# Moving the high parts of the weight ring, and the latents, by fractions of 256 bytes

## The chip, the cores and the metric

The kernel runs on one core of one Trainium2 chip. The metric is device time in microseconds (us) of one execution; lower is better. The time of a kernel is the median of its runs. The engines are named as in the profile: PE does the matmuls (PEld is its weight load), DVE, ACT and POOL are the vector, scalar and GpSimd engines, SP issues DMAs.

## The reference, cut to what matters

Two layers over 256 positions of width 1024. Layer 0 has latent attention, layer 1 has sparse attention over keys and values computed once between the layers. After each attention comes a PEER block: every position picks experts out of 16384 by product keys, and sums their outputs.

```python
def mla_mixer(x, ...):
    c_q  = rms_norm(proj[..., :512], q_norm)        # the latents
    c_kv = rms_norm(proj[..., 512:768], kv_norm)
    q, kv = c_q @ w_q_up, c_kv @ w_kv_up            # heads from the latents
    ...
def peer_ffn(x, w_q, subkeys, u, v):                # once in each layer
    q = x @ w_q                                     # 1024 -> 2048
    experts, g = top16(q, subkeys)                  # of 16384, 8 heads
    a = gelu(u[experts] . x)
    return sum(g * a * v[experts])
```

## The kernel before

**Arithmetic.** A float32 weight is used as the sum of a high part `hi` (float32 rounded to the format that PE multiplies in one pass, `F32R`) and a low part `lo = raw - hi`; so is the activation. A product is three matmuls: high by high, high by low, low by high.

**The stream.** All weights that pass through PE stand in one list, `plan()` (L50), in the order of use, as pieces of 128 rows by 1024 columns (the first eight by 800): projections of layer 0, then for each layer the queries of the PEER block (`p_wq`, 16 pieces), `p_u` (128 pieces) and `p_v` (128 pieces), and between the layers the weights of layer 1's attention. SP loads a piece into one of four places `raw` (in the v stage of both layers also into four places `spare`, which lie where the activations `hT` were). `_shi` (L111) lets ACT copy it into the next of four places of the ring `hi`, and `_slo` (L122) lets DVE subtract, into the next of four places of the ring `lo`. `nxt` hands the two to the matmuls; ACT and DVE work two pieces ahead of PE. Some pieces don't use the ring, but tiles of their own called `keep`.

**The stages of PE.** In the projections and in the *u stage* the weights are the stationary operand: `proj_T` (L198) runs, for each piece, 8 + 8 matmuls with blocks of 128 columns of `hi` and 8 with blocks of `lo`, against 256 columns of the activations `hT` as the moving operand. A u step (`u_step`, L708) does that for one piece. Once the expert choice is done (`if not side and len(A) == 1:`, L790), its buffers are freed, and the rest of the u steps are *wide*: 8 matmuls with `hi` against 512 columns (high and low half of `hT` in one), and 8 with `lo` against 256. There are 41 narrow and 87 wide steps in each layer. In the *v stage* the weights move (512 columns of `hi` or `lo`), and the gated activations `W` are stationary. Weights move also in the first projection, in the output projections (against `oT`), and in the first query pieces of each PEER block (against `hT`, `early_mm`). In `mla`, `proj_T` runs 192 matmuls of 256 columns with the latents `cT` as the moving operand.

**Where the tiles lie.** Tiles are laid one behind another in each partition's memory, each rounded up to 32 bytes, pool after pool. A place of the `hi` ring is 4096 bytes, and the four of them lie directly ahead of the four of `lo`. So modulo 256 bytes the starts are these: `hT` and `spare` 96; `raw`, all places of `hi`, all of `lo`, `W`, and the `keep` tiles of the v stage 160; the latents `cT`, and `qT`, `kT`, `vN`, `oT` of layer 0's attention 160; `oT` of layer 1's attention 224. All blocks that a matmul reads begin a multiple of 256 bytes behind these starts. Below, the *distance* of a matmul is the start of its moving operand less that of its weights, modulo 256: -64 for `hT` against `hi` or `lo`, 0 for `cT` against `hi`, 0 for `hi` against `W`, +64 where `hi` or `lo` moves against `hT`.

**The gather.** For 64 of the 256 positions, the last step of PEER is not done by PE: POOL gathers rows of `p_v` and DVE sums them in `g_mac` (L479), with the products of gate and activation in `gw`, made from `ggate`.

Of the kernel before, what the change touches and what calls it, by code (L numbers as in the profile page):

```python
# [12 lines left out]
F32 = mybir.dt.float32  # L13
F32R = mybir.dt.float32r
# [10 lines left out]
P = 128  # L25
# [18 lines left out]
class Kern:  # L44
# [5 lines left out]
    def plan(self):  # L50
        I, L = self.I, []
        self.v0s, self.spare, self.pairs = [], None, {}
        if "mla" in self.parts:
            L += [I["a_w_in"][k] for k in range(KC)]
            L += [I["a_wk"][i] for i in range(2)]
            L += [I["a_wq"][i] for i in range(3)]
            L += [I["a_wv"][i] for i in range(2)]
            L += [I["a_wq"][i] for i in range(3, 6)]
            L += [I["a_wo"][i] for i in range(KC)]
        for l in (0, 1):  # L60
            if l == 1 and "nsa" in self.parts:
                L += [I["s_wv"][i] for i in range(4)]
                L += [I["s_wT"][i] for i in range(4)]
                L += [I["b_wg"]]
                L += [I["s_wT"][i] for i in range(4, 8)]
                L += [I["b_wq"][i] for i in range(4)]
                L += [I["b_wq"][i] for i in range(4, 8)]
                L += [I["b_wo"][i] for i in range(KC)] + [I["b_wo"][i] for i in range(KC // 2)]
            if f"peer{l}" in self.parts:
                L += [I["p_wq"][l, i] for i in range(16)]  # L70
                L += [I["p_u"][l, (P - FIRST + j) % P] for j in range(P)]
                self.v0s.append(len(L))
                o = (len(L) - self.v0s[0]) % 4
                self.pairs.update((len(L) + j, I["p_v"][l, j:j + 2].rearrange("j i d -> i j d")) for j in range(o % 2, P - 1, 2))
                L += [I["p_v"][l, j] for j in range(P)]
        self.stream = L
        self.v0 = self.vb = self.v0s[0]
        self.si = 0
        self.sd = 0
        self.sh = 0  # L80
        self.sl = 0
        self.raws, self.his, self.los = {}, {}, {}
        self.share = False
        self.alt = {}
        self.later, self.now = [], 0
# [25 lines left out]
    def _shi(self, upto):  # L111
        while self.sh <= min(upto, len(self.stream) - 1):
            i = self.sh
            self._sdma(i, True)
            if i in self.alt:
                self.his[i], self.los[i] = self.alt.pop(i)()
            else:
                self.his[i] = self.shl.tile([P, self.raws[i].shape[-1]], F32R, tag="hi", name="hi")
            self.nc.scalar.copy(self.his[i], self.raws[i])  # L119
            self.sh += 1  # L120

# [320 lines left out]
    def peer(self, l):  # L442
        tc, nc, I = self.tc, self.nc, self.I
        self.v0 = self.v0s.pop(0)
        with ExitStack() as es:
# [14 lines left out]
            gat = pool(es, "gather")  # L460
            gidx = gat.tile([P, 2, P // 2], U32, name="gidx")
            ggate = gat.tile([P, P // 2], F32, name="ggate")
            gw = gat.tile([P, P // 2], F32, name="gw")
            gel = [gat.tile([P, 4], F32, name=f"gel{m}") for m in range(16)]
            gacc = gat.tile([P, D], F32, name="gacc")
            grow, gtable = {}, I["p_v"].rearrange("l j i d -> (l j i) d")
# [164 lines left out]
            def g_flush(n=1):  # L631
                if len(gq) < n:
                    return
                while gq:
                    t0, oi, gs = gq.popleft()
                    ps = self.acc(t0 // 4 % 2)
                    for q in range(4):
                        for w in range(2):
                            self.mm(ps[:, q * P:(q + 1) * P], oi[:, q // 2, :, q % 2], gs[w][:, q // 2, :, q % 2],
                                    w == 0, w == 1)  # L640
                    pv = ps.rearrange("p (t j) -> p j t", t=4)
                    k = done["a"]
                    for x, j0, n in A:
                        m = min(max(k, 0), n)
                        if m > 0:
                            y = x[:, 0:m, t0:t0 + 4]
                            nc.vector.scalar_tensor_tensor(y, pv[:, j0:j0 + m], 1.0 / GS, y, op0=OP.mult, op1=OP.mult)  # L647
                        if m < n:
                            nc.scalar.activation(x[:, m:n, t0:t0 + 4], pv[:, j0 + m:j0 + n], AF.Copy, scale=1.0 / GS)
                        k -= n  # L650
                    done["g"] = t0 + 4
# [41 lines left out]
            for n in range(4, 17):  # L693
                cur = []
                if n < 16:
                    hi, lo = self.nxt()
# [18 lines left out]
            def u_step(j):  # L715
                hi, lo = self.nxt()
                ps = self.ps()
                wide = len(A) > 1
                if wide:

                    def high(k):
                        self.mm(ps, hi[:, k * P:(k + 1) * P], self.hTT[:, k].rearrange("p a t -> p (a t)"), k == 0, k == KC - 1)

                    for k in range(KC - 1):
                        high(k)
                    for k in range(KC):
                        self.mm(ps[:, 0:S], lo[:, k * P:(k + 1) * P], xhi[:, k, :], False, False)
                    high(KC - 1)
                else:
                    self.proj_T(ps[:, 0:S], hi, lo, xhi, xlo, KC)  # L730
                return j, ps, wide
# [4 lines left out]
            def u_fin(x):  # L736
                while due:
                    y, ps = due.popleft()
                    nc.vector.tensor_tensor(y, y, ps, op=OP.mult)
                if x is None:  # L740
                    return
                j, ps, wide = x
                jj = (P - FIRST + j) % P
                y, n = slot(jj), done["g"]
                if wide:
                    t = gat.tile([P, S], F32, tag="half", name="half", bufs=2)
                    nc.scalar.copy(t, ps[:, S:2 * S])  # L747
                    nc.vector.tensor_tensor(ps[:, 0:S], ps[:, 0:S], t, op=OP.add)  # L748
                if n:
                    nc.scalar.activation(ps[:, 0:n], ps[:, 0:n], AF.Gelu)  # L750
                    due.append((y[:, 0:n], ps[:, 0:n]))
                if n < ND:
                    nc.scalar.activation(y[:, n:ND], ps[:, n:ND], AF.Gelu)  # L753
                if j % 4 == 0:
                    gst.append(gat.tile([P, 4, GT], F32, tag="gst", name="gst", bufs=2))
                nc.scalar.activation(gst[-1][:, j % 4, :], ps[:, ND:S], AF.Gelu)  # L756
                if j % 4 == 3:
                    nc.gpsimd.dma_start(self.actD[:, jj - 3:jj + 1, :], gst.pop())  # L758
                done["a"] = j + 1
# [24 lines left out]
            for j in range(P):  # L784
                x = u_step(j)
                u_fin(pu)
                pu = x
                g_flush(2)
                run_side(1.6 if len(A) == 1 else GB)
                if not side and len(A) == 1:  # L790
                    es_r.close()
                    hot = self.pr8.tile([P, 2, 3, 2, P, 2], F16, tag="r8", name="hot")
                    A.append((self.pr8.tile([P, NEXT, ND], F32, tag="r8", name="A2"), 0, NEXT))
                    n = P - FIRST - NEXT
                    A.append((pool(es_1, "slots1").tile([P, n, ND], F32, name="A1"), NEXT, n))
                    side.append(g_gen(hot))
                if done["g"] == ND and j >= P - 3 and not W:
                    w_start()
# [44 lines left out]
            for j in range(P):  # L843
# [9 lines left out]
                hi, lo = self.nxt(j < P - 2)  # L853
# [54 lines left out]
    def mla(self, hN, gb):  # L908
# [3 lines left out]
        with es:  # L912
            pool = lambda *a, **k: es.enter_context(tc.tile_pool(*a, reuse_waits="tile", **k))
            mp = pool(name="mla", bufs=1)
# [2 lines left out]
            keep = pool(name="mkeep", bufs=4)  # L917
            cN = mp.tile([P, 2, 768], F32, name="cN")
            kpN = mp.tile([P, 2, 32], F32, name="kpN")
            cT = [mp.tile([P, 6, S], F32R, tag=f"cT{i}", name=f"cT{i}") for i in range(2)]  # L920
            qT = mp.tile([96, NH, S], F32, name="qT")
            kT = mp.tile([96, NH, S], F32, name="kT")
            vN = mp.tile([P, 2, D], F32, name="vN")
            oT = [mp.tile([P, KC, S], F32R, tag=f"oT{i}", name=f"oT{i}") for i in range(2)]
            gq = mp.tile([P, 6], F32, name="gq")
            rN = mp.tile([P, 2, 64], F32, name="rN")
# [9 lines left out]
            for k in range(KC):  # L936
                hi, lo = self.nxt(k <= KC - 3)
# [66 lines left out]
            for b in range(2):  # L1004
                hi, lo = self.nxt(False)
# [14 lines left out]
            for b in range(2):  # L1020
                hi, lo = self.nxt()
# [21 lines left out]
            for k in range(2):  # L1043
                hi, lo = self.nxt()
# [14 lines left out]
            for st in range(NH + 3):  # L1059
# [20 lines left out]
                if 0 <= h < NH and h % 2 == 1:  # L1080
                    pvp = self.ps()
                    pp = [pts.pop(h - 1), pts.pop(h)]
                    for w in range(2):
                        for e in range(2):
                            o = pvp[64 * e:64 * e + 64, 0:S]
# [578 lines left out]
```

## Time and profile before

| what | us |
|---|---|
| median of 3 runs | 1758.89 (1757.74 to 1759.99) |
| the profiled execution | 1749.82 |
| its span, first to last instruction | 1748.0 |
| PE busy in it | 1703.1 (97%) |
| DVE busy | 1553.4 (89%) |
| ACT busy | 1042.9 (60%) |
| POOL busy | 481.4 (28%) |

The profiled execution is 9.1 us shorter than the median, and 1.8 us of it lie outside its span. A duration of a matmul in the profile is from its start to its end, and matmuls overlap: what one of them costs is the time from its start to the start of the next, its *pitch*. It is read from the timeline or the chain as the difference of two starts, divided by the number of matmuls between them.

### The profile page before, as it was taken

The numbers are of one execution on the slowest core, as the hardware profiler recorded it, in microseconds if no ns is written. First come the engines' busy times: TensorE is split into PE (matmuls) and PEld (weight loads), VectorE is DVE, ScalarE is ACT, GpSimd is POOL, SyncE is SP. The second block draws the span as 40 slices with busy tenths as digits, with TensorE's granted clock in tenths as the row PEclk, the third lists the DMA queues.
The fourth block names the chain that finished last, engine by engine and source line by source line (L and its number), as shares of the span: only waits on it lengthen the run. The fifth ranks groups of instructions, "written<-read, shape, count | busy, mean of one in ns | idle before, by whom it ended". The sixth has DMA issues, their size and how long they took to land.

```text
span 1748.0 us, 30707 instructions
## 1 busy us (share of the span) xinstructions
PE 1703.1 (97%) x10610; PEld 1478.1 (85%) x10610; DVE 1553.4 (89%) x3675; ACT 1042.9 (60%) x2267; POOL 481.4 (28%) x441
## 2 busy tenths in 40 slices
PE   7999999999999999999997999999999999999997
PEld 6879999888888788888785789998888888888886
DVE  5778988989998899999778789988899998999998
ACT  6646555766666555556466755556666666555554
POOL 2110002000001777761341210001000005777740
PEclk9999999999999999999999999999999999999999
DMA  7535667555556899999572265657555557999993
GB/s 246 169 128 195 193 204 261 186 178 181 187 183 251 309 391 370 367 360 332 179 268 67 95 206 176 205 184 275 176 181 186 184 183 290 401 383 369 361 363 110
DMA packets 118619, 416.66 MB, mean 238 GB/s; under 512 B 16032, under 2 KB 18112, under 8 KB 117376
## 3 DMA queue, kind: packets, MB, share of 16 engines
q1 hardware_dynamic: 88976, 322.60, 54.2%
q0 software_dynamic: 29488, 92.10, 14.1%
q8 instruction: 84, 1.38, 0.3%
q14 instruction: 71, 0.58, 0.1%
HBM read 400.49 MB, written 13.63 MB: 237 GB/s over the span
## 4 chain that ended last, share of the span: by engine, by line
PE 72%; issue 16%; DVE 6%; DMA 2%; ACT 2%; POOL 1%; SPq 0%; POOLq 0%; ACTq 0%; DVEq 0%
PE acc L196 36%; PE mm L196 35%; PE mm L223 1%; DVE lo L130 1%; DMA raw<-p_wq 1%; POOL actD L758 1%; DVE keep L130 1%; DMA xT<-xT 0%; POOL row L472 0%; ACT hi L119 0%; POOL gel L476 0%; DMA gel<-actD,gidx 0%; DVE gacc L486 0%; DVE W L774 0%; DMA actD<-gst 0%
## 5 line engine op out<-in xcount | busy, mean ns | idle before, releaser
L119 ACT CAST hi<-raw 128x1024 fp32r<-128x1024 f32 (+1 forms) x463 | 484.6, 1049 | 244.6 <-PE acc L196 99.8
L196 PE MATMUL mm<-hT,hi 128*128 128x256 f32 (+1 forms) x3360 | 612.8, 328 | 0.0
L130 DVE TENSOR_TENSOR lo<-raw,hi 128x1024 fp32r<-128x1024 f32 (+1 forms) x459 | 558.3, 1220 | 32.6 <-ACT hi L119 30.9
L196 PEld LDWEIGHTS mm<-hT,hi 128*128 128x128 f32 x3360 | 483.2, 188 | 46.3 <-issue 1.2
L196 PE MATMUL acc<-hi,W 128*128 128x512 f32 x1452 | 408.8, 390 | 0.0
L196 PEld LDWEIGHTS acc<-hi,W 128*128 128x128 f32 x1452 | 273.2, 188 | 57.0
L196 PEld LDWEIGHTS mm<-hT,lo 128*128 128x128 f32 x2376 | 306.7, 188 | 15.9
L196 PE MATMUL mm<-hT,lo 128*128 128x256 f32 x2376 | 320.0, 277 | 0.0
L196 PE MATMUL acc<-lo,W 128*128 128x512 f32 x968 | 299.6, 391 | 1.8 <-DVE lo L130 1.8
L758 POOL DMA_DIRECT2D actD<-gst x64 | 34.8, 544 | 783.9 <-ACT gst L756 783.9
L472 POOL DMA_INDIRECT row<-p_v,gidx x128 | 191.7, 1498 | 117.8 <-DVE gacc L486 79.9
L196 PEld LDWEIGHTS acc<-lo,W 128*128 128x128 f32 x968 | 181.7, 188 | 41.4 <-DVE lo L130 4.1
L119 ACT CAST hi<-spare 128x1024 fp32r<-128x1024 f32 x122 | 128.1, 1050 | 113.9 <-PE acc L196 100.8
L476 POOL DMA_INDIRECT gel<-actD,gidx x128 | 165.7, 1294 | 50.0 <-issue 36.6
L486 DVE SCALAR_TENSOR_TENSOR gacc<-row,gw,gacc 128x1024 f32<-128x1024 f32 x126 | 161.4, 1281 | 1.1
L130 DVE TENSOR_TENSOR lo<-spare,hi 128x1024 fp32r<-128x1024 f32 x122 | 148.8, 1220 | 5.4 <-ACT hi L119 4.5
L750 ACT ACTIVATE mm<-mm 128x192 f32<-128x192 f32 (+23 forms) x170 | 41.1, 242 | 122.4 <-DVE mm L748 122.4
L774 DVE TENSOR_TENSOR W<-A,W 128x128 fp32r<-128x128 f32 (+1 forms) x512 | 107.6, 252 | 1.8 <-ACT W L769 1.8
L748 DVE TENSOR_TENSOR mm<-mm,half 128x256 f32<-128x256 f32 x174 | 74.5, 428 | 15.4 <-ACT half L747 15.0
L769 ACT CAST W<-A 128x192 fp32r<-128x192 f32 x256 | 88.0, 345 | 0.0
L647 DVE SCALAR_TENSOR_TENSOR A<-acc,A 128x176 f32<-128x176 f32 (+16 forms) x268 | 56.1, 274 | 28.6 <-PE acc L196 25.6
L753 ACT ACTIVATE A<-mm 128x192 f32<-128x192 f32 (+23 forms) x244 | 67.3, 276 | 7.8 <-DVE mm L748 2.8
(275 smaller groups left out, 1759.1 us busy)
## 6 DMA issues: line engine op xcount, KB each, us to landing
raw<-p_u SPq DMA_DIRECT2D x256, 512.0 KB, 4.0
spare<-p_v SPq DMA_DIRECT2D x64, 1024.0 KB, 8.8
raw<-p_v SPq DMA_DIRECT2D x63, 1024.0 KB, 8.7
raw<-p_wq SPq DMA_DIRECT2D x32, 512.0 KB, 4.1
actD<-gst POOLq DMA_DIRECT2D x64, 128.0 KB, 3.9
raw<-b_wo SPq DMA_DIRECT2D x12, 512.0 KB, 3.8
raw<-a_wo SPq DMA_DIRECT2D x8, 512.0 KB, 4.6
raw<-s_wT SPq DMA_DIRECT2D x8, 512.0 KB, 5.6
```

The lines of the kernel that those rows point to most:

```text
L119: self.nc.scalar.copy(self.his[i], self.raws[i])
L130: e.tensor_tensor(self.los[i], raw, self.his[i].bitcast(F32), op=OP.subtract)
L196: self.nc.tensor.matmul(out, a, b, start=start, stop=stop)
L472: nc.gpsimd.indirect_dma_start(out=t, out_offset=None, in_=gtable, in_offset=bass.IndirectOffsetOnAxis(ap=gidx[:, 0, c:c + 1], axis=0))
L476: nc.gpsimd.indirect_dma_start(out=gel[c // 4][:, c % 4:c % 4 + 1], out_offset=None, in_=gplaces, in_offset=bass.IndirectOffsetOnAxis(ap=g ...
L486: nc.vector.scalar_tensor_tensor(gacc, t, gw[:, c:c + 1], gacc, op0=OP.mult, op1=OP.add)
L647: nc.vector.scalar_tensor_tensor(y, pv[:, j0:j0 + m], 1.0 / GS, y, op0=OP.mult, op1=OP.mult)
L748: nc.vector.tensor_tensor(ps[:, 0:S], ps[:, 0:S], t, op=OP.add)
L753: nc.scalar.activation(y[:, n:ND], ps[:, n:ND], AF.Gelu)
L758: nc.gpsimd.dma_start(self.actD[:, jj - 3:jj + 1, :], gst.pop())
L769: nc.scalar.copy(WW[j][:, 0:ND], slot(j))
L774: nc.vector.tensor_tensor(WW[j][:, o:o + c.stop - c.start], slot(j)[:, c], WW[j][:, c].bitcast(F32), op=OP.subtract)
```

## The change

The tile of a place in the `hi` ring becomes 32 columns (128 bytes) longer: 4224 bytes are 16.5 times 256, so the four places start at 160, 32, 160 and 32 modulo 256. Everything behind the ring moves by 512 bytes, and keeps its start modulo 256. A piece may be put 32 columns into its place, by a table `odd`: for a piece in it with value 1, the pieces all start at 160; with value 0, all at 32; for a piece that is not in it, at the place's own start. The 128 v pieces of each layer get 1. When layer 1's u stage becomes wide, its remaining u pieces get 0. All others (projections, layer 0's u, layer 1's narrow u) alternate between 160 and 32. The ring `lo` stays at 160.

In layer 0's attention a pad of 64 bytes ahead of `cT` moves `cT`, `qT`, `kT` and `vN` to 224, and one of 192 bytes behind them puts `oT` and what follows back to 160. To make room, `gw` is `ggate` itself: the product is written over the gate.

No instruction is added or taken away, and none changes its shape, its order or its engine.

```diff
@@ plan
         self.v0s, self.spare, self.pairs = [], None, {}
+        self.nh, self.odd = 0, {}
...
                 o = (len(L) - self.v0s[0]) % 4
+                self.odd.update((len(L) + j, 1) for j in range(P))
@@ _shi
             else:
-                self.his[i] = self.shl.tile([P, self.raws[i].shape[-1]], F32R, tag="hi", name="hi")
+
+                n = self.raws[i].shape[-1]
+                o = 32 if self.nh % 2 == self.odd.get(i) else 0
+                self.nh += 1
+                self.his[i] = self.shl.tile([P, n + 32], F32R, tag="hi", name="hi")[:, o:o + n]
@@ peer
-            gw = gat.tile([P, P // 2], F32, name="gw")
+            gw = ggate
...
                 if not side and len(A) == 1:
                     es_r.close()
+                    if l == 1:
+                        self.odd.update((i, 0) for i in range(self.si, self.v0))
@@ mla
             kpN = mp.tile([P, 2, 32], F32, name="kpN")
+            mp.tile([P, 16], F32, name="pad")
             cT = [mp.tile([P, 6, S], F32R, tag=f"cT{i}", name=f"cT{i}") for i in range(2)]
...
             vN = mp.tile([P, 2, D], F32, name="vN")
+            mp.tile([P, 48], F32, name="pad2")
```

## Rows read from the trace of the kernel before

**Rows 1.** The page: engines' busy time (share, instructions), and the chain by engine.

```profile
PE 1703.1 (97%) x10610; PEld 1478.1 (85%) x10610; DVE 1553.4 (89%) x3675; ACT 1042.9 (60%) x2267; POOL 481.4 (28%) x441
...
PE 72%; issue 16%; DVE 6%; DMA 2%; ACT 2%; POOL 1%; SPq 0%; POOLq 0%; ACTq 0%; DVEq 0%
```

**Rows 2.** Stretches: length, busy us (instructions) by engine, clock; narrow, wide, v.

```profile
172.00:259.70 87.70, 87.70 (x774) 87.70 (x775) 82.72 (x340) 48.80 (x100) 3.79 (x7) 1.00 0.65 203
285.60:550.60 265.00, 265.00 (x1778) 231.28 (x1777) 239.55 (x588) 172.27 (x482) 16.88 (x27) 1.00 0.60 196
560.00:840.00 280.00, 277.99 (x1216) 228.78 (x1215) 266.61 (x455) 160.35 (x248) 174.51 (x125) 0.99 0.92 346
```

**Rows 3.** PE's longest waits: total us, times, longest us.

```profile
PE acc L196 <- ACT hi L119: 7.2, 2, 6.5
PE mm L223 <- DVE p L1555: 4.2, 4, 1.7
```

**Rows 4.** Timeline of PE, wide u step: start us, length, matmuls, count.

```profile
330.99 2.02 PE L196 MATMUL mm<-hT,hi 128*128 128x512 f32 x8
332.85 1.07 PE L196 MATMUL mm<-hT,lo 128*128 128x256 f32 x8
333.76 2.02 PE L196 MATMUL mm<-hT,hi 128*128 128x512 f32 x8
```

**Rows 5.** Timeline of PE in layer 0's v stage.

```profile
660.47 0.61 PE L196 MATMUL acc<-lo,W 128*128 128x512 f32 x2
660.92 0.62 PE L196 MATMUL acc<-hi,W 128*128 128x512 f32 x2
661.38 0.62 PE L196 MATMUL acc<-lo,W 128*128 128x512 f32 x2
661.83 1.07 PE L196 MATMUL acc<-hi,W 128*128 128x512 f32 x4
662.74 0.62 PE L196 MATMUL acc<-lo,W 128*128 128x512 f32 x2
663.19 0.61 PE L196 MATMUL acc<-hi,W 128*128 128x512 f32 x2
```

**Rows 6.** Timeline of PE where weights move against `hT`, 512 columns.

```profile
860.27 3.83 PE L196 MATMUL acc<-lo,hT 128*128 128x512 f32 x16
863.94 0.75 PE L196 MATMUL mm<-hT,hi 128*128 128x256 f32 x5
```

**Rows 7.** The same, 288 columns.

```profile
22.91 0.43 PE L196 MATMUL acc<-hi,hT 128*128 128x288 f32 x2
23.18 0.29 PE L196 MATMUL acc<-lo,hT 128*128 128x288 f32 x1
23.31 0.43 PE L196 MATMUL acc<-hi,hT 128*128 128x288 f32 x2
23.57 0.29 PE L196 MATMUL acc<-lo,hT 128*128 128x288 f32 x1
23.71 0.53 PE L196 MATMUL acc<-hi,hT 128*128 128x288 f32 x2
```

**Rows 8.** Chain in time, runs of narrow steps: start us, us, count.

```profile
171.92 87.77 PE mm L196 x772
...
864.10 24.55 PE mm L196 x216
...
1155.87 25.44 PE mm L196 x216
```

**Rows 9.** Timeline of PE, matmuls on the latents.

```profile
31.15 0.64 PE L196 MATMUL mm<-cT,hi 128*128 128x256 f32 x4
...
33.31 0.27 PE L223 MATMUL mm<-ident,kpN 128*32 128x128 f32 x1
```

**Rows 10.** Groups by form: matmuls by operands, and DVE's subtraction; count, busy us, mean ns.

```profile
L196 PE MATMUL mm<-hT,hi 128*128 128x512 f32 x1392 | 364.1, 397 | 0.0
L196 PE MATMUL mm<-hT,hi 128*128 128x256 f32 x1968 | 248.6, 279 | 0.0
L130 DVE TENSOR_TENSOR lo<-raw,hi 128x1024 fp32r<-128x1024 f32 x451 | 550.7, 1224 | 29.7 <-ACT hi L119 28.1
L130 DVE TENSOR_TENSOR lo<-spare,hi 128x1024 fp32r<-128x1024 f32 x122 | 148.8, 1220 | 5.4 <-ACT hi L119 4.5
```

## The prediction

> **What bounds the kernel now.** The page comes first: PE is busy for 97% of the span, and the chain that ended last runs over PE for 72% and over "issue" for 16% [rows 1]. Then the table of stretches. In narrow and wide u steps PE is busy for the whole length, at a granted clock of 1.00 (the 2.4 GHz level), while DVE, the next one, is busy for 82.72 of 87.70 and 239.55 of 265.00 us [rows 2]. The longest wait of PE's in the whole execution is 7.2 us in two pieces [rows 3]. So in these stages a nanosecond of a matmul's pitch is a nanosecond of the end, and DVE leaves room for a faster PE: 5 us in the narrow stretch, 25 in the wide.
>
> The third view is the timeline, for pitches, set beside the addresses. The wide step runs 8 matmuls of 512 columns from 330.99 to 332.85, 232.5 ns each, at distance -64 [rows 4]. The v stage runs 12 of the same width from 660.47 to 663.19: 226.7 ns, at distance 0 [rows 5]. Sixteen that move `lo` against `hT`, at +64, take 3.67 us: 229.4 ns [rows 6]. Same columns, same weight loads, same clock: what differs between the three is the distance. For 256 columns, a run of 772 narrow matmuls (-64) takes 113.7 ns each, and so does one of 216; another run of 216 at the same distance takes 117.8 [rows 8]. So at -64 there are two rhythms, 113.7 and 117.8, and the longer can last for nine steps. The latents, at distance 0, go from 31.15 to 33.31 with 18 matmuls, of which the rows show the first and the end: 120.0 ns [rows 9]. I read this as the weight load and the running matmul getting in each other's way, by their places modulo 256 bytes. In the v stage DVE and ACT work beside PE all the time and the pitch stays at 226.7, so other engines are not the cause.
>
> **The change part by part.**
>
> *Wide u steps.* For `hi` at 32 the distance becomes 96 - 32 = +64. There are 696 such matmuls in each layer, 1392 in both [rows 10]. In layer 0 half of the steps get it, 348 matmuls; in layer 1 all but the two or three pieces already placed, about 680. Together some 1030. Their nearest row has the same distance and width with the roles exchanged, 229.4 ns [rows 6]: 1030 x (232.5 - 229.4) = **-3.2 us**. Bounds: 226.7, the lowest pitch seen at 512 columns, would make it -6.0; no gain if the sign of the distance doesn't matter, 0. I take the row with the same distance.
>
> *Narrow steps and projections.* Of 1968 matmuls of 256 columns with `hi` [rows 10] half, 984, go from -64 to +64. No row shows 256 columns at +64. The nearest are two. At 288 columns and +64, 6 matmuls from 22.91 to 23.71 take 133 ns [rows 7]; by the v stage's pace (226.7 x 288 / 512 = 127.5) that is 5.5 too much. At 256 columns and -64, 113.7 is what that pace gives (113.4): nothing too much [rows 8]. Above, the latents' 120.0 bounds it [rows 9]: 984 x 6.3 = +6.2 us. Below, only the 117.8 rhythm can go: if changing starts pulled every such stretch to 113.7, the run of 216 [rows 8], its like in layer 0 and about as many in the query projections would give 4.1 ns x some 800 = -3.3 us. I take **0**: a run of 256 columns has no free time between weight loads, as the run at -64 that finds its undisturbed rhythm and keeps it, and unlike 288 columns, where each load begins anew. Ends kept: -3.3 and +6.2.
>
> *Latents.* 192 matmuls leave distance 0 (120.0 ns) for -/+64; at the usual 113.7 that is 192 x 6.3 = **-1.2 us**; bounds 0 and -1.2.
>
> *The rest.* In v the starts are what they were: 0. Where `hi` moves, half of some 260 matmuls change their distance; at 6 ns either way +/-0.8 us, taken as 0. `vN` against the probabilities, 64 matmul passes, +/-0.4, taken as 0. `gw` over `ggate` keeps reader and writer on DVE, in the same order: 0. ACT's and DVE's work on `hi` at 32: the subtraction takes 1224 ns with `raw` (160) and 1220 with `spare` (96) beside the same `hi` [rows 10], so two inputs 64 bytes apart or alike are the same to it; DVE's slack above covers that, and without it 573 subtractions would cost 0.6 us per ns.
>
> **Sum**: -3.2 + 0 - 1.2 = -4.4 us. The rows are of an execution of 1749.82 us, 9.1 below the median; the difference is carried over whole: 1758.9 - 4.4 = **1754.5 us**.
>
> **A rule that speaks against it.** In the rows, 512 columns take 226.7 or 232.5 ns as the operands stand [rows 4, 5]. The Trainium skill says otherwise, on its page "TensorE: Matmul & The Clock Gate", "Part 2: What happens when you issue a matmul": PE has two independent read ports, and "Loading the next tile's weights doesn't steal SBUF read bandwidth from the running matmul." By that rule no start modulo 256 could matter, and the sum would be 0; the trace disagrees by those 5.8 ns.
>
> **The rivals.** *Nothing comes of it* (1758.9): either the three pitches come from something that goes with the stage and not with the distance (which operand moves, how runs follow one another), or the narrow steps lose what the wide win: 984 x 4.5 = 4.4, a pitch of 118.2 at +64. For it: no row shows `hi` as weights at two starts. Against it: -64, 0 and +64 give three pitches at one width.
>
> *All of the disturbance goes* (1748.4): 512 columns fall to 226.7 (-6.0), the 117.8 rhythm vanishes (-3.3), latents -1.2: -10.5 us. For it: 226.7 exists at distance 0. Against it: the one row at +64 is 229.4.
>
> *Slower* (about 1764): the 117.8 rhythm. Within a changed step the weights now jump from 32 (`hi`) to 160 (`lo`) and back, which happens nowhere today, and each jump may throw the stream out of the 113.7 rhythm, the step after it too. There are some 2900 matmuls of 256 columns in narrow steps and projections; all at 117.8 where now about 800 are, that is 2100 x 4.1 = +8.6 us; with the latents' pitch (120.0) in the 984, another 2.2. With -3.2 and -1.2 the sum is +4.2 to +6.4, near 1764. It decides from about 1100 more matmuls at 117.8 on, where the sum is zero. For it: that rhythm exists and holds for nine steps. Against it: 772 matmuls in a row stay at 113.7 though their steps end in other matmuls, and run back.
>
> **How the numbers follow.** Forecast 0.50 (1754.5), nothing 0.20, all gone 0.16, slower 0.14. About 0.2% (3.5 us) is what a measurement of this kernel can tell from no change. The forecast lies just beyond it, so I count 0.38 of its 0.50 as faster and 0.12 as the same: faster 0.54, same 0.32, slower 0.14. The range goes down to the full gain, 1748.4, and up to 1761, where the narrow steps lose all of their bound beside the other two terms (+6.2 - 3.2 - 1.2 = +1.8, 1760.7). The slower case stays outside.
>
> **What would show it.** Right: in the timeline of layer 1's wide steps 8 `hi` matmuls take 1.83 instead of 1.86 us, in layer 0 every second step does; the latents' 18 take 2.05 instead of 2.16; the chain's narrow runs stay near 113.7; the v stage is unchanged at 226.7. Wrong: wide steps of layer 1 still at 232.5 (the distance isn't it); narrow runs at 118 or more in every second step (the loss that I set to 0); DVE's or ACT's durations on `hi` changed; or PE waiting where it did not.

## The result, and the profile after

The changed kernel takes 1746.59 us (median of 6 runs, 1744.64 to 1751.13), against 1758.32 us for the kernel before beside it: a ratio of 0.9939, 95% interval 0.9919 to 0.9959. By that ratio it is some 10.7 us faster; the two medians differ by 11.7. The forecast was 4.4 less, and 1746.59 lies below the range's lower end of 1748.4. Two repetitions, below, gave 0.9950 and 0.9938.

The page of the changed kernel: span, busy time, the chain by engine.

```profile
span 1749.4 us, 30707 instructions
...
PE 1701.7 (97%) x10610; PEld 1479.0 (85%) x10610; DVE 1553.1 (89%) x3675; ACT 1043.6 (60%) x2267; POOL 480.6 (27%) x441
...
PE 69%; issue 16%; DVE 7%; DMA 4%; ACT 2%; POOL 2%; SPq 0%; POOLq 0%; ACTq 0%; DVEq 0%
```

This is the first thing to learn here: the traced execution after has a span of 1749.4 us, *longer* than the 1748.0 of the one before, while the medians differ the other way. A page against a page shows no gain. The page after belongs to the slowest of its kernel's six executions (1751.13), the page before to one that was 9.1 below its median. Between layer 0's v stage and layer 1's narrow steps, with layer 1's attention, the trace after is 4.4 us longer (226.4 us from 844.8 on, against 222.0 from 846.2 on), at a granted clock of 0.96 against 0.98. So the stages have to be compared one by one, over several traces.

Stretches of the changed kernel, with the limits of [rows 2]: length, busy us (instructions) of PE, PEld, DVE, ACT, POOL, clock, and its two longest runs of narrow steps in the chain.

```profile
172.00:259.70 87.70, 87.69 (x772) 87.50 (x771) 83.91 (x342) 49.35 (x101) 3.80 (x7) 1.00 0.63 199
285.60:550.60 265.00, 264.44 (x1783) 231.66 (x1782) 240.56 (x588) 172.43 (x484) 18.47 (x28) 1.00 0.60 197
```

```profile
173.11 87.95 PE mm L202 x772
...
1070.77 87.95 PE mm L202 x772
```

PE is as full and its clock the same. A narrow run of 772 matmuls takes 113.9 ns each, hardly other than the 113.7 of [rows 8]. The timeline, in a wide step of layer 0 with the high parts at 160, one with them at 32, and one of layer 1 at 32:

```profile
332.07 2.02 PE L202 MATMUL mm<-hT,hi 128*128 128x512 f32 x8
333.94 1.07 PE L202 MATMUL mm<-hT,lo 128*128 128x256 f32 x8
334.85 2.00 PE L202 MATMUL mm<-hT,hi 128*128 128x512 f32 x8
336.68 1.07 PE L202 MATMUL mm<-hT,lo 128*128 128x256 f32 x8
...
1299.64 2.00 PE L202 MATMUL mm<-hT,hi 128*128 128x512 f32 x8
1301.47 1.07 PE L202 MATMUL mm<-hT,lo 128*128 128x256 f32 x8
```

Eight take 1.87 us at distance -64 (from 332.07 to 333.94) and 1.83 at +64: 233.8 and 228.8 ns, against 232.5 of [rows 4]. (The timeline rounds to 0.01 us, which is 1.3 ns here; over all such steps of layer 0's wide stage the means are 232.7 and 229.4.) The distance acts as forecast, within one stage, from one step to the next. The latents and the v stage:

```profile
31.33 0.63 PE L202 MATMUL mm<-cT,hi 128*128 128x256 f32 x4
...
33.45 0.38 PE L229 MATMUL mm<-ident,kpN 128*32 128x128 f32 x2
```

```profile
659.92 0.62 PE L202 MATMUL acc<-lo,W 128*128 128x512 f32 x2
660.37 1.07 PE L202 MATMUL acc<-hi,W 128*128 128x512 f32 x4
661.28 0.62 PE L202 MATMUL acc<-lo,W 128*128 128x512 f32 x2
661.73 0.61 PE L202 MATMUL acc<-hi,W 128*128 128x512 f32 x2
662.18 0.62 PE L202 MATMUL acc<-lo,W 128*128 128x512 f32 x2
```

The 18 matmuls on the latents take 2.12 us, 117.8 ns each, where [rows 9] have 120.0. In v ten take 2.26 us, 226 ns as in [rows 5]. DVE's subtraction and PE's wide matmuls, grouped by form, with mean durations of 1223 and 396 ns, are hardly other than in [rows 10]:

```profile
L136 DVE TENSOR_TENSOR lo<-raw,hi 128x1024 fp32r<-128x1024 f32 x451 | 550.3, 1223 | 32.7 <-ACT hi L125 31.3
...
L202 PE MATMUL mm<-hT,hi 128*128 128x512 f32 x1392 | 361.2, 396 | 0.0
```

So the wide steps gain what they should, and these rows show little else. Where do the other 7 us come from?

### The profile page after: what moved, and what is told of

Read it like the earlier page. It is cut to its first block, busy times and chain, and to the rows that moved or that the text cites. A ratio compares the mean times of both kernels' runs of the same rounds, so it can differ in the third digit from the quotient of the medians.

```text
span 1749.4 us, 30707 instructions
## 1 busy us (share of the span) xinstructions
PE 1701.7 (97%) x10610; PEld 1479.0 (85%) x10610; DVE 1553.1 (89%) x3675; ACT 1043.6 (60%) x2267; POOL 480.6 (27%) x441
## 4 chain that ended last, share of the span: by engine, by line
PE 69%; issue 16%; DVE 7%; DMA 4%; ACT 2%; POOL 2%; SPq 0%; POOLq 0%; ACTq 0%; DVEq 0%
PE acc L202 35%; PE mm L202 33%; DVE lo L136 1%; PE mm L229 1%; DMA actD<-gst 1%; POOL row L478 1%; DMA raw<-p_wq 1%; POOL actD L764 1%; ACT hi L125 1%; DVE keep L136 1%; DMA raw<-s_wT 0%; DMA xT<-xT 0%; DVE gacc L492 0%; POOL gel L482 0%; DVE W L780 0%
## 5 line engine op out<-in xcount | busy, mean ns | idle before, releaser
L125 ACT CAST hi<-spare 128x1024 fp32r<-128x1024 f32 x122 | 128.2, 1051 | 112.5 <-PE acc L202 99.8
L482 POOL DMA_INDIRECT gel<-actD,gidx x128 | 161.6, 1262 | 49.5 <-issue 34.7
L492 DVE SCALAR_TENSOR_TENSOR gacc<-row,ggate,gacc 128x1024 f32<-128x1024 f32 x126 | 161.3, 1280 | 1.1
```

Source lines behind the costliest of these rows:

```text
L482: nc.gpsimd.indirect_dma_start(out=gel[c // 4][:, c % 4:c % 4 + 1], out_offset=None, in_=gplaces, in_offset=bass.IndirectOffsetOnAxis(ap=g ...
L492: nc.vector.scalar_tensor_tensor(gacc, t, gw[:, c:c + 1], gacc, op0=OP.mult, op1=OP.add)
```

## The experiments

**Theory A, the rhythm:** in most executions of the kernel before, more narrow matmuls run at 117.8 ns than in the one whose trace was read; the change takes them out of it. **Theory B, the distance alone:** as the prediction has it. **Theory C, chance:** the gain is spread of the runs. The four kernels first run are the kernel before again, and the change in its parts. The diffs show the lines that matter, against the changed kernel unless another is named. Wherever the ring is longer or `hT` is padded, `gw` is `ggate`, to make room. Each ratio is to the kernel before, run beside it.

**The kernel before, four times more** (no edit).

> The kernel before, a second time, for its trace and the spread of its times. The profiled execution of before took 1749.82 us, 9 below its median of 1758.89, and the changed kernel's 1751.13, 4.5 above its own of 1746.59, so the two traces are not typical of the two medians. Theory A (rhythm): in most executions of before, more of the 256-column matmuls run at 117.8 ns instead of 113.3; then a second trace near the median shows longer narrow runs (87.77 us would become up to 91) and the difference of 9 us lies there, up to 4.4 ns x 2100 = 9 us. Theory B (pitch by distance alone, that is the prediction): the matmul pitches are the same in every execution, and the difference to the first trace lies in waits outside the u stages (start, loads after layer 0, attention). Theory C (chance): the median comes out nearer 1750 and the gain was noise.

> The kernel before once more, for a trace. If the term that was missed is the share of narrow matmuls at 117.8 ns, its narrow stages take one of the values 112.2, 113.2, 115.6 or 116.6 us (neither, the short, the long or both uninterrupted runs at 117.8), more of them long than in the first trace, and its span goes with them.

> As the one before it: narrow stages of 112.2, 113.2, 115.6 or 116.6 us. If all come out at 113.2 as in the first trace, the narrow term cannot explain the gain.

> As the one before it. Over the traces in which all narrow weights stand at 160, a mean narrow stage of 115 us or more would account for 5 us of the gain in both layers against the 112.5 of the changed kernel.

The first: ratio to itself 0.9992 (0.9974 to 1.0010), 12 runs, median 1760.88. The others have one run each: 1750.62, 1756.84 and 1757.20. The chain of the second (1750.62) and of the third (1756.84), their runs of narrow steps:

```profile
171.84 87.77 PE mm L196 x772
...
1068.49 87.77 PE mm L196 x772
1156.59 25.44 PE mm L196 x216
```

```profile
171.18 91.17 PE mm L196 x772
...
1071.48 91.17 PE mm L196 x772
1162.98 25.44 PE mm L196 x216
```

The same 772 matmuls take 87.77 us or 91.17: 113.7 or 118.1 ns each. (From start to start it is 113.5 or 117.9; the chain also counts the end of the last matmul. Below, these two are called the 113.4 and the 117.8 rhythm.) The spans of the two differ by 6.3 us, the chain's two runs by 6.8. Each narrow stage has one uninterrupted run of 32 steps, and one of nine. Between them PE transposes what the choice of experts made, and each run of steps begins in one rhythm or the other, and in this kernel *stays in it to its end*. Counted over the ten narrow stages of the five traces of before, the long run is at 117.8 in six, and the short in five. The long runs of the two layers agree in each trace, so it is rather a matter of the execution: three of five had both at 117.8. Theory A stands; the trace that the prediction read had both long runs at 113.4, and both short ones at 117.8.

From the starts in the traces, the length of the four u stages, in us (narrow: from the first step of the long run to the first wide step):

| kernel | layer 0 narrow | layer 0 wide | layer 1 narrow | layer 1 wide |
|---|---|---|---|---|
| before, trace read for the prediction | 113.2 | 265.1 | 113.2 | 265.1 |
| before again | 115.6 | 265.5 | 115.6 | 266.1 |
| second, third, fourth repetition | 113.2, 115.6, 115.6 | 265.9, 266.3, 265.4 | 113.2, 116.6, 115.6 | 265.1, 265.1, 265.2 |
| changed kernel | 112.6 | 264.7 | 112.6 | 263.7 |
| changed kernel, two repetitions | 112.6, 112.6 | 264.0, 264.4 | 112.6, 112.6 | 263.2, 263.6 |
| wide steps only | 115.6 | 263.5 | 115.6 | 264.0 |
| narrow steps only | 112.4 | 265.6 | 112.6 | 265.6 |
| latents only | 115.6 | 265.4 | 116.6 | 265.1 |
| high parts at 32 throughout, twice | 112.5, 112.3 | 263.3, 263.2 | 112.5, 112.5 | 263.4, 264.1 |
| activations moved to 224 | 116.6 | 264.4 | 116.6 | 264.4 |
| activations moved to 160 | 118.7 | 266.6 | 118.7 | 266.6 |
| one piece in eight | 112.7 | 265.1 | 113.2 | 265.1 |
| low parts moved | 112.2 | 267.8 | 113.2 | 267.8 |

**The wide steps alone.**

```diff
-                o = 32 if self.nh % 2 == self.odd.get(i) else 0
+                o = 32 if self.nh % 2 == self.odd.get(i, 1) else 0
...
-                    if l == 1:
-                        self.odd.update((i, 0) for i in range(self.si, self.v0))
+                    self.odd.update((i, 0) for i in range(self.si, self.v0))
```

(and no pads in `mla`)

> Only the wide u steps of both layers have their high parts at 32 (distance +64); projections, narrow steps and latents as before. Theory B: 1392 matmuls at 229 instead of 232.5 ns, 1392 x 3.5 = 4.9 us faster than before, and nothing more. Theory A: the same 4.9 us or a little more, since the narrow steps keep their rhythm; well short of the whole 11 us. Theory C: within 1 us of before.

Ratio 0.9976 (0.9957 to 0.9995), some 4.2 us: the 4.9 that theories A and B both expect lies in the interval. In its table row only the wide stages are shorter than before; the narrow ones are at 115.6.

**The narrow steps and projections alone.**

```diff
-                    if l == 1:
-                        self.odd.update((i, 0) for i in range(self.si, self.v0))
+                    self.odd.update((i, 1) for i in range(self.si, self.v0))
```

(and no pads in `mla`)

> Only projections and narrow u steps alternate between 160 and 32; the wide steps and v stay at 160, the latents as before. Theory B: no gain, 0 to +6 us by the bounds of the prediction. Theory A: this holds most of the gain, 5 to 8 us faster than before, and in its trace the narrow runs stay near 113.4 ns. Theory C: within 1 us of before.

Ratio 0.9962 (0.9940 to 0.9984), some 6.7 us. Theory B has nothing here; A has 5 to 8. Both of its long runs in the chain are at 113.9 ns, as in the changed kernel:

```profile
171.17 87.95 PE mm L202 x772
...
1065.99 87.95 PE mm L202 x772
```

**The latents alone** (the kernel before with the two pads only).

> Only the two pads in layer 0's attention: the latents at 224 instead of 160, the high parts as before. Theories A and B: 192 matmuls at 114 to 117 instead of 120 ns, 0.6 to 1.2 us, which these rounds can hardly tell from nothing. A larger gain would mean that the distance isn't what counts in the latents' stretch.

Ratio 1.0012 (0.9996 to 1.0028): no gain that the runs could show. The parts' 4.2 and 6.7 add up to the whole, as far as their intervals (0.9 to 7.6 and 2.8 to 10.6 us) can tell; both lie clear of zero, and theory C falls with them.

**What ends the 117.8 rhythm?** Must the start differ from step to step, or is a change inside a step enough? First without any alternation:

```diff
-                o = 32 if self.nh % 2 == self.odd.get(i) else 0
+                o = 32 if self.nh % 2 == self.odd.get(i, 0) else 0
...
-                    if l == 1:
-                        self.odd.update((i, 0) for i in range(self.si, self.v0))
```

> All high parts at 32 in projections and in all u steps (nothing alternates from step to step); low parts at 160, v and latents as in the changed kernel. Two theories of what keeps the narrow steps at 113.3 ns. Theory S (step to step): the start must differ from one step to the next; then a run that begins at 117.8 stays there, narrow stages take 112.4 to 116.6 us by chance as in before, and the kernel is 3 to 6 us slower than the changed one, but the wide stages take 263.6. Theory I (inside the step): a change of distance between high and low parts, here +64 to -64 in every step, is enough; then narrow stages stay at 112.4 us and the kernel is equal to the changed one or 1 us faster. The prediction's own fear, 120 ns at +64, would show as narrow stages of 117 us or more.

> High parts at 32 in projections and all u steps of both layers, beside the changed kernel: 0.8 us less in layer 0's wide stage and 0.1 in each narrow one, so within 0.1% of it. A difference of 0.2% or more would mean that alternating itself does something that the stages of one trace don't show.

Ratios 0.9955 (0.9938 to 0.9972) and 0.9933 (0.9917 to 0.9949), the second beside the changed kernel's 0.9938. The narrow stages stay at 112.3 to 112.5 us though nothing alternates: theory S (the start must differ from one step to the next) falls, and so does the fear of 120 ns at +64 *in this setting*. As a version it equals the change, and is simpler. (The first of its traces is not typical: 1744.22 us, against a median of 1753.39. The second, 1744.64, lies at its median of 1744.87.)

Then one distance for all, in the kernel before, with the activations moved:

```diff
             self.pers = pers
+            pers.tile([P, 32], F32, name="pad")
             self.new_hT()
+            pers.tile([P, 32], F32, name="pad2")
```

> The kernel before with the activations hT (and spare) moved by 128 bytes to 224, and nothing else: high and low parts all stand at +64 from hT, and nothing alternates. Distance alone: wide matmuls with 512 columns at 229 instead of 232.5 ns, 1392 x 3.5 = 4.9 us less, narrow at 113.3 to 117.8 by chance as before; 0.2 to 0.4% faster than before. If +64 itself holds the narrow steps at 113.3 the gain is 9 to 11 us, the whole of the change's; if +64 is bad at 256 columns (120 ns), narrow stages take 117 us or more.

Ratio 1.0013 (0.9997 to 1.0029). High and low parts are all at +64 now. The wide stages gain about 1 us each, and the narrow ones are at 117.9 throughout, a step of 24 from 186.04 to 188.87 taking 2.83 us:

```profile
186.04 2.05 PE L196 MATMUL mm<-hT,hi 128*128 128x256 f32 x16
187.93 1.10 PE L196 MATMUL mm<-hT,lo 128*128 128x256 f32 x8
188.87 2.05 PE L196 MATMUL mm<-hT,hi 128*128 128x256 f32 x16
```

So +64 alone holds nothing at 113.4. The pitch is that of the longer rhythm at -64, so a single trace could be chance; the runs say that it is not. With narrow stages as they fell in the five traces of before, the 2.1 us that the wide stages gain would have given a ratio of 0.9988, below the interval. So it looks as if the *change* between two distances helped. The same with 64 bytes less, at distance 0 (pads of 16 and 48 columns):

> The kernel before with the activations hT and spare moved by 64 bytes, to 160: distance 0 from all weights in projections and u. If the pitch goes by the distance, 512 columns take 226.7 ns as in v (1392 x 5.8 = 8 us less) and 256 columns 120 ns as on the latents (some 2950 in narrow steps and projections, 1392 in wide ones: 4340 x 4 to 6.5 = 17 to 28 us more), 0.5 to 1.2% slower in all. If 120 ns belongs to the latents for another reason, it is up to 8 us faster.

Ratio 1.0093 (1.0076 to 1.0110), 16 us longer:

```profile
187.63 2.08 PE L196 MATMUL mm<-hT,hi 128*128 128x256 f32 x16
189.55 1.12 PE L196 MATMUL mm<-hT,lo 128*128 128x256 f32 x8
...
337.54 2.00 PE L196 MATMUL mm<-hT,hi 128*128 128x512 f32 x8
339.38 1.11 PE L196 MATMUL mm<-hT,lo 128*128 128x256 f32 x8
```

Sixteen of 256 columns take 1.92 us, 120.0 ns each, as on the latents. Eight of 512 take 1.84 us, 230 ns, not 226.7: among matmuls of 256 columns at 120, the v stage's pitch isn't reached, and the 8 us that the expectation set against the loss mostly did not come.

**One changed step in eight.**

```diff
+                self.odd.update((len(L) + j, 0) for j in range(4, P, 8))
                 L += [I["p_u"][l, (P - FIRST + j) % P] for j in range(P)]
```

(all others at 160, wide and v too; no pads)

> The kernel before with one u piece in eight (4, 12, 20, 28, 36 of the narrow ones) at 32 and all other pieces at 160; wide, v, projections, latents as before. If a change of distance takes the matmuls from the 117.8 ns rhythm to 113.3 and they stay there afterwards, one changed step is enough: a narrow stage is long only up to its first changed step, at most 5 of 32 and 5 of 9 steps, 240 matmuls at 117.8, and takes 112.2 to 113.4 us, where before takes 113.2 to 116.6 by chance; 2 to 6 us faster than before. If each step needs its own change, seven steps of eight stay at 117.8 in the runs that begin so: 115 to 116 us, no gain.

Ratio 0.9963 (0.9949 to 0.9978), as much as the 0.9962 with all narrow steps changed. The timeline around the first changed step, whose `hi` starts at 183.16:

```profile
180.34 2.05 PE L203 MATMUL mm<-hT,hi 128*128 128x256 f32 x16
182.22 1.10 PE L203 MATMUL mm<-hT,lo 128*128 128x256 f32 x8
183.16 2.04 PE L203 MATMUL mm<-hT,hi 128*128 128x256 f32 x16
185.04 1.09 PE L203 MATMUL mm<-hT,lo 128*128 128x256 f32 x8
185.97 1.98 PE L203 MATMUL mm<-hT,hi 128*128 128x256 f32 x16
187.78 1.07 PE L203 MATMUL mm<-hT,lo 128*128 128x256 f32 x8
```

The changed step's 16 matmuls at +64 still take 1.88 us (117.5 ns), and so did the step ahead of it. Then PE goes on to the low parts at -64, and the next step's 16 take 1.81 us: 113.1. Start by start, the low parts of the changed step are 116, 123, 118, 114, 113, 113, 114, 113 ns. From there the run keeps 113.4 to its end. In the three runs of steps that began at 117.8 in this trace the turn came at just this border, from 16 matmuls at +64 to the low parts at -64; one change is enough.

The changed kernel's own trace shows the same border. Its long run begins with the high parts at 160, and its second step has them at 32:

```profile
173.57 2.13 PE L202 MATMUL mm<-hT,hi 128*128 128x256 f32 x16
175.54 1.10 PE L202 MATMUL mm<-hT,lo 128*128 128x256 f32 x8
176.48 2.04 PE L202 MATMUL mm<-hT,hi 128*128 128x256 f32 x16
178.37 1.09 PE L202 MATMUL mm<-hT,lo 128*128 128x256 f32 x8
179.29 1.98 PE L202 MATMUL mm<-hT,hi 128*128 128x256 f32 x16
181.10 1.07 PE L202 MATMUL mm<-hT,lo 128*128 128x256 f32 x8
```

The first step takes 123 and 117.5 ns, the high parts of the second 118, its low parts 115, and the third step 113.1. So the change does not keep the runs from beginning at 117.8: in its three traces all twelve runs of steps begin so, and all twelve leave that rhythm in their second step. In the other kernels with moved high parts, five runs began at 113.4 and stayed there through changed steps (one of them here): no border was seen to lead back. Nor does every such border lead out: with all high parts at 32, three short runs passed the first one at 117.8 and turned at the second.

**The mirror: the low parts moved, the high ones at 160.**

```diff
-                self.los[i] = self.shl.tile([P, raw.shape[-1]], F32R, tag="lo", name="lo")
+                n = raw.shape[-1]
+                o = 32 if self.nl % 2 == self.odd.get(i, 0) else 0
+                self.nl += 1
+                self.los[i] = self.shl.tile([P, n + 32], F32R, tag="lo", name="lo")[:, o:o + n]
```

(against the kernel before; the v pieces stay at 160)

> The mirror: the high parts as before at 160 (distance -64), the low parts at 32 (+64) in projections and all u steps, at 160 in v. If a change of distance inside the step is what counts, whichever part moves, narrow stages take 112.4 us as with the high parts moved; the wide steps keep 512 columns at -64, 265 us; 4 to 6 us faster than before. If it must be the high parts at +64, narrow stages are 113.2 to 116.6 us by chance and nothing is gained.

Ratio 0.9996 (0.9984 to 1.0008): neither expectation, since both had the wide stages at 265 us. In the trace, three of four runs of steps were at 113.4, but they began so; the one that began at 117.8, nine steps long, stayed there although the distance changes twice in each step. So "any change of distance, every time" is too much said. And the wide stages are 2.2 and 2.5 us longer than the means of before, since 8 low matmuls at +64 take 0.94 us instead of 0.91. These 4.6 us together would make a ratio of 1.0026 if the narrow stages fell as in the traces of before; the interval ends below that, so most of the runs probably had shorter narrow stages, as the trace has (112.2 and 113.2 us). Whether the moved low parts do that or chance, one trace can't show: the mirror is not settled. The step where its low matmuls are read:

```profile
331.69 2.02 PE L201 MATMUL mm<-hT,hi 128*128 128x512 f32 x8
333.55 1.11 PE L201 MATMUL mm<-hT,lo 128*128 128x256 f32 x8
334.49 2.03 PE L201 MATMUL mm<-hT,hi 128*128 128x512 f32 x8
```

**Wide steps of both layers at +64; and at 0 and +64 in turn.** The first has the switch without `if l == 1:`, the second also this:

```diff
-                o = 32 if self.nh % 2 == self.odd.get(i) else 0
+                o = 32 if self.nh % 2 == self.odd.get(i) else 16 if self.odd.get(i) == 0 else 0
```

> The changed kernel with the high parts at 32 in the wide steps of both layers, not of layer 1 alone. By the pitch at +64, 348 more matmuls at 229 instead of 232.5 ns: layer 0's wide stage 263.6 instead of 264.7 us, 1.1 us faster than the changed kernel, 0.67% faster than before. If layer 0's wide stage stays at 264.7, the distance isn't what counts there.

> The changed kernel with the wide steps of both layers at 96 (distance 0) and 32 (+64) in turn. If distance 0 gives 226.7 ns to 512 moving columns wherever they come from, as in v, the wide steps at 96 save 2.3 ns on each of 672 matmuls against +64: wide stages of 262.8 us each, 1.6 us faster than with both at +64 and 2.7 faster than the changed kernel. If distance 0 delays the weight load itself (the latents' 120 ns at 256 columns), the last wide matmul of a step or the first of 256 columns behind it pays, and nothing is left.

The first: 0.9954 (0.9925 to 0.9982), with layer 0's wide stage at 263.6 us instead of 264.0 to 264.7, as expected; the time cannot tell it from the change. The second: 0.9949 (0.9930 to 0.9968), wide stages of 264.3 and 264.8 us, against 263.6 and 264.0 in the first, so distance 0 gives nothing more there. From start to start, its low matmuls, of 256 columns, take 116.0 ns on average instead of 114.2, and lose more than the high ones win (229.1 instead of 229.5).

**The v stage.** The change keeps all high parts at 160 there. Without that line they alternate between 160 and 32, at distances 0 and 128 from `W`:

```diff
-                self.odd.update((len(L) + j, 1) for j in range(P))
```

> The changed kernel, but the high parts alternate in v too: half of the moving high parts stand at distance 128 (32 - 160) from W, the rest at 0. If 0 is the best distance for weights that move (226.7 ns against 229 to 236 at other distances), about 640 matmuls lose 2 to 6 ns each: the v stages get 1.3 to 3.8 us longer together and the kernel 0.1 to 0.2% slower than the changed one. If distance matters only for the weights' load, nothing.

Ratio 0.9982 (0.9966 to 0.9998): more than half of the gain is given back, measured by the 0.9954 of the kernel above that ran beside it with v at 160 (the intervals overlap a little; the pitch bears it out). Ten matmuls from 661.37 to 663.67 take 230 ns each instead of 226, and its two v stages 297.5 and 289.1 us, against 286.1 and 284.8 in the changed kernel's first trace. Not all of the first 11.4 is the pitch: in layer 0's v stage, after PE had been busy for 7.1 of 9.2 us, its granted clock fell to 0.50 (the 1.2 GHz level) for a while, which the changed kernel's first trace doesn't have there. Layer 1's stage had no such fall, and lost 4.3 us. That is more than the 1.3 to 3.8 us expected for both, because the low parts, at distance 0 as ever, got longer as well. Here an even distance is worth more than the best one half of the time.

```profile
661.37 1.08 PE L201 MATMUL acc<-hi,W 128*128 128x512 f32 x4
662.29 0.62 PE L201 MATMUL acc<-lo,W 128*128 128x512 f32 x2
662.75 0.62 PE L201 MATMUL acc<-hi,W 128*128 128x512 f32 x2
663.20 0.63 PE L201 MATMUL acc<-lo,W 128*128 128x512 f32 x2
663.67 1.09 PE L201 MATMUL acc<-hi,W 128*128 128x512 f32 x4
```

The stretch with the fall, in the form of [rows 2]:

```profile
589.20:596.00 6.80, 6.05 (x14) 4.06 (x14) 3.51 (x8) 3.77 (x7) 2.23 (x2) 0.50 0.97 366
```

**The changed kernel again.**

> The changed kernel a second time, beside the others: 0.5 to 0.7% faster than before; its trace has narrow stages of 112.4 to 112.6 us, a first wide stage of 264.7 and a second of 263.7, and what else differs from its first trace lies in v and in layer 1's attention, where two executions of one kernel differ as well.

> The changed kernel a third time. The runs of before beside the last experiments had a median of 1747.8 us, those beside the earlier ones 1754.6 to 1761.2, so the gain may differ from one set to another. If it comes from the share of narrow matmuls at 117.8 ns in before (0 to 980 of 982 per layer, 0 to 9 us) and from the wide steps (2.8 us), it lies between 0.15 and 0.65% in every set, largest where before is slowest; the changed kernel's own stages stay at 112.6, 264.4, 112.6 and 263.6 us.

Ratios 0.9950 (0.9933 to 0.9967) and 0.9938 (0.9921 to 0.9954). All six narrow stages of its three traces are 112.6 us.

## Why the prediction was wrong, point by point

- *What bounds the kernel*: right. PE stays full in the u stages, and a pitch goes straight into the time. DVE's room was enough.
- *Wide steps, -3.2 us*: right, in direction and size. Over three traces after and five before, the wide stages went from 265.6 to 264.4 and from 265.3 to 263.5 us: -3.1. At +64 the wide steps run at 229.4 ns on average, just what the row with the roles exchanged had said. That a row of another stage gave the size is in part luck: at distance 0 the v stage's 226.7 did not carry over to the u stage, which takes 230 there. And at 256 columns one distance has two pitches, so the distance alone doesn't fix the pitch.
- *Narrow steps and projections, 0 us*: **the term that failed.** The means over the same traces are 114.6 to 112.6 and 114.8 to 112.6: -4.3 us; the kernel with this part alone was 6.7 us faster by its runs. The prediction named the 117.8 rhythm, and put its price at -3.3 at most, but counted its matmuls in the one trace it had, some 800, where both long runs happened to be at 113.7, and carried the sum over to the median whole. In three of five executions the two long runs are at 117.8 as well: 1544 matmuls more, 6.8 us in the chain. And the term was set to 0 on the ground that a run finds its undisturbed rhythm and keeps it; the changed kernel's runs begin in the disturbed one, and leave it in their second step. The traced execution was 9.1 us below the median, which the prediction said and did not ask about; by the means some 3 us of it were this.
- *Which way a jump works*: the rival "slower" had it the wrong way round. A jump of the start does not throw the stream out of the 113.4 rhythm; from +64 to -64, behind 16 matmuls, it brings it in, at the first or second such border in every traced run of u steps that began at 117.8. The pitch of 118.2 at +64, by which the rival *nothing* priced the narrow steps, shows where all weights are at +64 (117.9). It isn't paid where the low parts stay at -64: with all high parts at +64 the narrow stages are at 112.3 to 112.5 us.
- *Latents, -1.2 us*: a little too much. The first 18 went from 120.0 to 117.8, not to 113.7. Over all 192, leaving out starts more than 135 ns apart, the mean went from 119.9 in the trace before to 115.4, 114.7 and 116.0 in three after: 0.7 to 1.0 us, which no run could show.
- *v and the rest, 0*: right for v, pitch for pitch.
- *The rule of the skill*: the Trainium skill's page "TensorE: Matmul & The Clock Gate", "Part 2: What happens when you issue a matmul", has the weight load on a read port of its own, which takes no read bandwidth from the running matmul. The prediction read it so that no start could matter. The runs disagree with that: moving `hT` (and `spare`) by 128 and by 64 bytes, with no instruction changed, took the narrow matmul to 117.9 and 120.0 ns, and no run of steps at -64 shows 120.0. That the two reads get in each other's way is still the prediction's guess: the runs show that the starts matter, not how.

The traces place -7.4 us in the u stages; the runs say 10.7, 8.8 and 10.9, with intervals down to 7.2, 5.8 and 8.1. The rest, 1 to 3 us, isn't settled: the v stages of the traces differ by 1.9 in the means, but between executions of one kernel by up to 6.6. Something beside the rhythm moves whole executions, too. With the narrow steps alone changed, twelve runs range from 1750.9 to 1763.4 us, with a gap between 1753.6 and 1759.4, and only the shortest of them was traced. In the trace with the wide steps of both layers at +64 the v stages are 8.3 and 3.4 us longer than in the changed kernel's second trace; what sets such executions apart isn't known. Nor is it shown what sets the rhythm with which a run of steps begins, or how the border from +64 to -64 ends it. In one group of runs the kernel before had a median of 1747.8 us, about the changed kernel's own elsewhere; what the change gives there was not measured.

## What to carry to other kernels

One trace is one draw: where an execution lies 9 us off the median, find out which stage that is before a sum is built on it. A run of like matmuls can settle in one of two rhythms and keep it for tens of microseconds, so look at its first steps and not only at its mean; a small irregularity in the operands' starts, once in eight steps, was enough to end the worse one. Starts modulo 256 bytes of moving operand and weights are worth a look where PE is full; measure each width and each stage, since the distance that was best at 512 columns was not at 256.

## What the runs showed of the hardware

- At 256 columns the pitch is 113.4 or 117.8 ns at distance -64, both with the same instructions and addresses; 117.9 where all weights are at +64; 120.0 where all are at 0. At 512 columns among others of 256 it is 232.7 on average at -64, 229.4 at +64 and 230.1 at 0; in v, at 0 throughout, 226.7, and 230 where every second high part stands 128 bytes off.
- In the traces of the kernel before, each rhythm lasted for the whole of an uninterrupted run, up to 772 matmuls, while ACT and DVE worked beside it. In the changed kernel's three traces all twelve runs went from the longer to the shorter one in their second step.
